# Filler tiles that shift the byte offsets of a mixer layer's matrix operands, on one Trainium2 core

## Chip, core and metric

The kernel runs on one core of a Trainium2 chip. The metric is the device time of one execution in microseconds (us). Engines are named as the profile names them: PE is TensorE's matmul, PEld its weight load, DVE VectorE, ACT ScalarE, POOL GpSimd, SP SyncE, which issues most of the transfers.

## What is computed

The reference is one decoder layer on x of 1024 tokens by 1024 channels, all float32:

```python
h = rms_norm(x, g_pre) * (1.0 + scale) + shift
proj = h @ w_in                      # 1024 x 7704, split into 13 parts
o_fox  = fox_attention(fq, fk, fv, log_f)      # 8 heads of 64, causal, forget gates
o_gla  = rms_norm(gla_chunked(gq, gk, gv, log_a))   # 4 heads, carried state
o_pool = pool_mixer(pu, w_pool, pool_scale)    # windows 2, 4, 8, 16
y_b = (o_b * silu(z_b)) @ w_br_b               # for each of the three branches
merged = sigmoid(m_fox) * y_fox + sigmoid(m_gla) * y_gla + sigmoid(m_pool) * y_pool
out = x + gate * rms_norm(merged @ w_out, g_post)
```

## The kernel before

Each matrix is split into a rounded high part and the rest (`split`, ACT for the high part, DVE for the rest). A product is then three matmuls: high by high, high by low, low by high. `mm3` issues these three for one 128-row slice of the contraction. The first operand of a matmul here is the stationary one, which a weight load (PEld) brings into the array ahead of each matmul; the second is the moving one, streamed as 512 columns in most products.

The stages, in order, with the names that the profile shows for the PSUM tile:

- the start: normalise, transpose and modulate x into `hh` and `hl` (high and low part of h, transposed), with the first products `ps_gq`, `ps_gk`, `ps_n` in between;
- gated linear attention with its projections. `proj_N256` makes tiles `ps_gv` and `ps_fv` of 256 columns, `proj_T` makes tiles of 512 columns (`ps_gq`, `ps_gk`, and `ps_zg` for the first part of z_gla);
- 23 pairs of 128-channel column groups of `w_in` through `seven`, a scheme with seven block products instead of eight. A pair's tiles are `pp_zg`, `pp_pu`, `pp_zp`, `pp_fq`, `pp_fk`, `pp_zf` or `pp_m`; each of its seven products is four slices by three matmuls, so a pair has 84 matmuls of 128x512, and all pairs 1932. The weights `w_*` are prepared by POOL sums (`S_*`), ACT and DVE splits; the moving operands are `hh`, `hl` and the sums `T2`, `T3`, `T4`. Between them, pooling windows (`win`) and the small products `pspl` hang on DVE;
- attention in 128-query blocks (`psL`, `tp`, `po`), with the first branch product `psy` of y_pool woven in;
- `y_tile` for the branches (`psy`, 3 x 192 matmuls of 128x512), then the output product `pso` (360 of 512 columns, 48 of 256) and the final norm.

SBUF tiles lie in pools that are opened and closed as stacks from the left and from the right end of each partition, so a tile's byte offset follows from the sizes of what was opened before it on its side. Left: `cst`, `wp` (weights of `proj_T` and `proj_N256`), `hp` (`hh`, `hl`), `tq`, `tr` (the sums T); later `mA`, `yp` (branch weights `wh_y`, `wl_y`), `oga` (operands `ogh`, `ogl` of two branches), `wo` (`woh`, `wol`). Right: `shr` (the weights `w_*` of `seven`, the attention operands), and later `ogf` and `mB` (operands of the third branch, `ml`). A scheduler sets the order of instructions on each engine from a model of their durations.

Of the kernel before, what the change touches and what calls it, by code (L numbers as in the profile page):

```python
# [8 lines left out]
F32 = mybir.dt.float32  # L9
# [7 lines left out]
P = 128  # L17
# [12 lines left out]
def kernel(  # L30
# [22 lines left out]
    V, A, G, T = nc.vector, nc.scalar, nc.gpsimd, nc.tensor  # L53

    def pool(name, bufs=1, side="left", space=None):
        kw = dict(name=name, bufs=bufs, reuse_waits="tile")
        if space is not None:
            kw["space"] = space
        else:
            kw["side"] = side  # L60
        return tc.tile_pool(**kw)

    def open_pool(name, **kw):
        stack = ExitStack()
        return stack.enter_context(pool(name, **kw)), stack
# [7 lines left out]
    def halves():  # L73
        return ((0, slice(0, HALF)), (1, slice(HALF, S)))


    cst = ctx.enter_context(pool("cst"))
# [4 lines left out]
    def bank(tag, name, shape=(P, HALF)):  # L82
        if tag == "acc":
            return ps_acc.tile(list(shape), F32, tag="acc", name=name, bufs=2)
        return ps_acc.tile(list(shape), F32, tag=tag, name=name, bufs=BANKS[tag])
# [21 lines left out]
    def split(raw, hi, lo, scale=1.0, E=None):  # L107
        i = A.activation(hi, raw, AF.Copy, scale=scale)  # L108
        if scale == 1.0:
            j = (E or V).tensor_tensor(out=lo, in0=raw, in1=hi.bitcast(F32), op=ALU.subtract)  # L110
        else:
            j = V.scalar_tensor_tensor(
                out=lo, in0=raw, scalar=scale, in1=hi.bitcast(F32), op0=ALU.mult, op1=ALU.subtract
            )
        return i, j
# [14 lines left out]
    def load_w_256(src, name):  # L130
        parts = []
        for kh in range(2):
            rows = src[kh * 512 : (kh + 1) * 512, :].rearrange("(k p) e -> p k e", p=P)
            raw = wtile("wr", f"wr_{name}{kh}", F32, (P, 4, 256))
            nc.sync.dma_start(raw, rows)
            hi, lo = (wtile(t, f"{t}_{name}{kh}", shape=(P, 4, 256)) for t in ("wh", "wl"))
            split(raw, hi, lo)
            parts.append((hi, lo))
        return parts

    def mm3(ps, wh, wl, rh, rl, first, last):
        T.matmul(ps, wh, rh, start=first, stop=False)  # L142
        T.matmul(ps, wh, rl, start=False, stop=False)  # L143
        T.matmul(ps, wl, rh, start=False, stop=last)  # L144
# [12 lines left out]
    def proj_N256(col, name, evac):  # L157
        parts = load_w_256(w_in[0, :, col : col + 256], name)
        for st in range(S // P):
            sl = slice(st * P, (st + 1) * P)  # L160
            ps = ps_acc.tile([P, 256], F32, tag="acc", name=f"ps_{name}{st}")
            for k in range(NK):
                wh, wl = parts[k // 4]
                wh, wl = wh[:, k % 4, :], wl[:, k % 4, :]
                T.matmul(ps, hh[k][:, sl], wh, start=(k == 0), stop=False)  # L165
                T.matmul(ps, hh[k][:, sl], wl, start=False, stop=False)  # L166
                T.matmul(ps, hl[k][:, sl], wh, start=False, stop=(k == NK - 1))
            with tc.high_priority():
                evac(st, ps)


    shr, shr_stack = open_pool("shr", side="right")
# [323 lines left out]
    for i in range(3):  # L496
        t = gp.tile([P, 4, 2, 64], F32, tag=f"qbd{i}", name=f"qbd{i}")
# [3 lines left out]
    for i in range(2):  # L501
        t = gp.tile([P, 4, P], F32, tag=f"scs{i}", name=f"scs{i}")
# [180 lines left out]

    gates(0)
    proj_N256(C_GV, "gv0", evac_vg(0))
    gla_unit(0, 0)
    proj_T(C_GQ + P, "gq1", evac_q(1))
    proj_T(C_GK + P, "gk1", evac_k(1))
    gates(1)
    forget_logs()  # L690
    gla_unit(0, 1)
    proj_N256(C_FV, "fv0", evac_vf(0))
    proj_N256(C_GV + 256, "gv1", evac_vg(1))
    rms_gla(0)
    gla_unit(1, 0)
# [14 lines left out]
    sp, sp_stack = open_pool("seven", side="right")  # L710
# [161 lines left out]
    def big(name, dt=F32):  # L872
        brot[0] += 1
        return sh(GT[brot[0] % 2], name, dt=dt)

    def parts_to_dram(t, hi_d, lo_d, name, scale=1.0, hi=None):
        if hi is None:
            hi = big(f"hi_{name}", F32R)
        split(t, hi, t.bitcast(F32R), scale)
        nc.sync.dma_start(hi_d, hi.bitcast(F32))  # L880
        nc.sync.dma_start(lo_d, t)
# [41 lines left out]
    def fin_pool(q, d):  # L923
        def f(j, t):
            g = 2 * q + j
            raw = sp.tile([P, P], F32, tag="wpr", name=f"wpr{g}")
            nc.sync.dma_start(raw, w_pool[0, g])
            wph = sp.tile([P, P], F32R, tag="wph", name=f"wph{g}")
            wpl = sp.tile([P, P], F32R, tag="wpl", name=f"wpl{g}")
            split(raw, wph, wpl)  # L930
            dh, dl = big(f"dh{g}", F32R), big(f"dl{g}", F32R)
            split(d[j], dh, dl)
            for i, hs in halves():
                ps = bank("bd"[i], f"pspl{g}{i}")
                mm3(ps, wph, wpl, dh[:, hs], dl[:, hs], True, True)
                V.scalar_tensor_tensor(out=t[:, hs], in0=ps, scalar=psc[:, g : g + 1], in1=t[:, hs],
                                       op0=ALU.mult, op1=ALU.mult)
            parts_to_dram(t, oph_dram[g], opl_dram[g], f"op{g}")
        return f
# [116 lines left out]
    mA, mA_stack = open_pool("mA")  # L1056
    yp, yp_stack = open_pool("yp")
    oga, oga_stack = open_pool("oga")

    def load_y(src, name):  # L1060
        raw = yp.tile([P, NK, P], F32, tag="wr", name=f"wr_{name}", bufs=2)
        nc.sync.dma_start(raw[:, 0:4, :], src.rearrange("(k p) e -> p k e", p=P))
        hi = yp.tile([P, 4, P], F32R, tag="wh", name=f"wh_{name}", bufs=2)
        lo = yp.tile([P, 4, P], F32R, tag="wl", name=f"wl_{name}", bufs=2)
        split(raw[:, 0:4, :], hi, lo, 0.25)
        return hi, lo
# [157 lines left out]
        y_tile(1, j, "mid", ("d", "b") if j == 8 - KEEP else ("a", "c"))  # L1224
    oga_stack.close()
    wo, wo_stack = open_pool("wo")
    woh, wol = [], []

    def load_wo(k2, n):
# [83 lines left out]
```

## Time and profile before

| what | value |
|---|---|
| median of 3 runs | 1142.23 us (1141.19 to 1147.51) |
| the profiled execution | 1150.32 us, span 1148.6 us |
| PE busy | 1096.8 us, 95% of the span |
| PEld / DVE / ACT / POOL busy | 870.5 / 768.4 / 456.3 / 403.8 us |
| mean granted clock of PE | 0.978 |

A matmul's own duration (some 0.39 us for 512 columns) is longer than the time from its start to the start of the next, since matmuls overlap; the pace is read from starts.

### The profile page before, as it was taken

To read this page: it belongs to the slowest core of one execution; us is meant where nothing else is said; L and a number is where in the kernel's file an instruction comes from. 1 tells how busy PE (TensorE), PEld (TensorE's weight loads), DVE (VectorE), ACT (ScalarE), POOL (GpSimd) and SP (SyncE) were. 2 spreads that over 40 slices of the span, in tenths; PEclk is the share of its full clock that TensorE was granted. 3 is DMA by queue.
4 is the path that set the end of the run, shared out by engine and by line. 5 is a ranking of instruction groups with operands and counts; after the bars stand their busy time and mean duration, and the time that the engine had idled before them with its cause. 6 is when DMAs were issued, how large, how long until landed. Compare 5 with 4: busy or idle time off the path is not lost.

```text
span 1148.6 us, 15822 instructions
## 1 busy us (share of the span) xinstructions
PE 1096.8 (95%) x5812; PEld 870.5 (76%) x5812; DVE 768.4 (67%) x1427; ACT 456.3 (40%) x864; POOL 403.8 (35%) x348
## 2 busy tenths in 40 slices
PE   6899997999998999899999999998998999999997
PEld 4579786988886888688888888875675777677886
DVE  7667799767778677987666564536564668477323
ACT  5235354434534332443434443324443444433211
POOL 4323235033454345445645454411020225343000
PEclk9799999999998999999999999998999999999999
DMA  9810111211332433256653333289949584465332
GB/s 290 227 38 20 37 42 34 65 52 52 116 109 94 149 124 97 74 201 239 220 181 113 128 110 112 88 247 309 234 148 230 182 242 138 165 201 166 110 110 74
DMA packets 109746, 159.81 MB, mean 139 GB/s; under 512 B 7842, under 2 KB 83164, under 8 KB 109668
## 3 DMA queue, kind: packets, MB, share of 16 engines
q1 hardware_dynamic: 109316, 157.99, 45.1%
q8 instruction: 46, 0.75, 0.3%
q10 hardware_dynamic: 352, 0.80, 0.2%
q14 instruction: 32, 0.26, 0.1%
HBM read 113.64 MB, written 45.12 MB: 138 GB/s over the span
## 4 chain that ended last, share of the span: by engine, by line
PE 77%; DVE 11%; DMA 6%; POOL 2%; issue 2%; ACT 2%; SPq 0%; DVEq 0%; ACTq 0%; POOLq 0%
PE pp_m L142 7%; PE pp_m L143 7%; PE pp_m L144 7%; PE po L1105 3%; PE psy L142 3%; PE psy L144 3%; PE psy L143 3%; PE pso L1264 3%; PE pso L1265 3%; PE pso L1263 3%; PE tp L1095 3%; DMA wr_y<-in_w_br_pool_dram 2%; PE psc L605 2%; PE ps_gv L165 1%; PE ps_gv L166 1%
## 5 line engine op out<-in xcount | busy, mean ns | idle before, releaser
L999 POOL TENSOR_SCALAR_AFFINE_SELECT Fd<-F 128x128 f32<-128x128 f32 x64 | 22.9, 359 | 163.4 <-DVE mx L1021 122.6
L143 PE MATMUL psy<-ogl,wh_y 128*128 128x512 f32 x192 | 77.0, 401 | 3.0 <-DMA ogl<-opl_d 3.0
L142 PE MATMUL psy<-ogh,wh_y 128*128 128x512 f32 x192 | 78.0, 410 | 0.4 <-DMA ogh<-oph_d 0.3
L143 PE MATMUL pp_m<-hl,w_m 128*128 128x512 f32 x192 | 75.9, 396 | 0.0
L144 PE MATMUL pp_m<-hh,w_m 128*128 128x512 f32 x192 | 75.9, 396 | 0.0
L142 PE MATMUL pp_m<-hh,w_m 128*128 128x512 f32 x192 | 75.9, 395 | 0.0
L144 PE MATMUL psy<-ogh,wl_y 128*128 128x512 f32 x192 | 75.1, 400 | 0.1
L1028 ACT ACTIVATE t<-t,ng 128x1024 f32<-128x1024 f32 (+3 forms) x64 | 49.6, 776 | 53.6 <-DVE ng L1026 52.4
L110 DVE TENSOR_TENSOR w_m<-wr_m,w_m 128x512 fp32r<-128x512 f32 x36 | 45.1, 1256 | 28.1 <-ACT w_m L108 28.1
L110 DVE TENSOR_TENSOR w_m<-S_m,w_m 128x512 fp32r<-128x512 f32 x48 | 53.9, 1150 | 5.3 <-ACT w_m L108 4.9
L516 POOL TENSOR_TENSOR e<-cum 128x256 f32<-128x256 f32 x24 | 19.9, 829 | 103.1 <-ACT ek L575 30.7
L1095 PE MATMUL tp<-ident,t 128*128 128x128 f32 x288 | 48.8, 286 | 6.8 <-ACT PT L1097 6.7
L1016 DVE CUSTOM_DVE_ANT_0 t<-psL,F 128x512 f32<-128x512 f32 (+2 forms) x80 | 41.0, 523 | 19.9 <-PE psL L1013 14.9
L1264 PE MATMUL pso<-wol,mh 128*128 128x512 f32 (+1 forms) x136 | 51.8, 382 | 0.0
L1265 PE MATMUL pso<-woh,ml 128*128 128x512 f32 (+1 forms) x136 | 51.7, 382 | 0.0
L903 ACT ACTIVATE o_m<-o_m 128x512 f32<-128x512 f32 x48 | 29.1, 630 | 56.5 <-DVE o_m L804 41.4
L1263 PE MATMUL pso<-woh,mh 128*128 128x512 f32 (+1 forms) x136 | 51.4, 379 | 0.0
L1095 PEld LDWEIGHTS tp<-ident,t 128*128 128x128 f32 x288 | 33.8, 143 | 22.3 <-ACT PT L1097 10.4
L1267 DVE TENSOR_TENSOR yo<-pso,gb 128x512 f32<-128x512 f32 (+1 forms) x17 | 11.2, 661 | 55.4 <-ACT jk L1266 55.4
L1105 PE MATMUL po<-PT,vf 128*64 128x256 f32 (+1 forms) x320 | 48.0, 373 | 0.0
L771 POOL TENSOR_TENSOR S_m<-wr_m,wr_m 128x512 f32<-128x512 f32 x12 | 15.6, 1296 | 86.1 <-DMA wr_m<-in_w_in_dram 86.1
L143 PEld LDWEIGHTS psy<-ogl,wh_y 128*128 128x128 f32 x192 | 36.5, 190 | 11.7 <-DMA ogl<-opl_d 4.5
(580 smaller groups left out, 3417.7 us busy)
## 6 DMA issues: line engine op xcount, KB each, us to landing
wr_m<-in_w_in_dram SPq DMA_DIRECT2D x24, 512.0 KB, 4.2
m_d<-o_m SPq DMA_DIRECT2D x24, 512.0 KB, 4.8
m_in<-m_d SPq DMA_DIRECT2D x24, 512.0 KB, 5.5
wa<-in_w_ada_dram SPq DMA_DIRECT2D x16, 512.0 KB, 7.5
xn<-in_x_dram SPq DMA_DIRECT2D x8, 512.0 KB, 6.2
kl<-fkl_d SPq DMA_DIRECT2D x16, 256.0 KB, 10.4
kk<-fkh_d SPq DMA_DIRECT2D x16, 256.0 KB, 6.6
F<-fc_d SPq DMA_DIRECT2D x8, 512.0 KB, 10.3
```

The costliest lines, as they stand in the source:

```text
L110: j = (E or V).tensor_tensor(out=lo, in0=raw, in1=hi.bitcast(F32), op=ALU.subtract)
L142: T.matmul(ps, wh, rh, start=first, stop=False)
L143: T.matmul(ps, wh, rl, start=False, stop=False)
L144: T.matmul(ps, wl, rh, start=False, stop=last)
L903: A.activation(t, t, AF.Tanh, scale=0.5)
L1016: V.tensor_tensor_reduce(out=t[:, c0:e], in0=ps[:, : e - c0], in1=Fb[p, h][:, c0:e], scale=1.0, scalar=-3e38, op0=ALU.subtract, op1=ALU.ma ...
L1028: A.activation(t[:, :W], t[:, :W], AF.Exp, bias=ng[:, 0:1], accum_out=sm)
L1095: T.transpose(tp[:, j, :], t[:, kb * P : (kb + 1) * P], ident)
L1105: T.matmul(po[64 * h : 64 * h + 64, q0:256], vf[p // 2, kb // 4][:, kb % 4, col : col + 64], pts[h, kb // 4][:, kb % 4, q0:256], start=(kb ...
L1263: T.matmul(ps[:, :w], mh[k][:, sl], hi, start=(k == 0), stop=False)
L1264: T.matmul(ps[:, :w], mh[k][:, sl], lo, start=False, stop=False)
L1265: T.matmul(ps[:, :w], ml[k][:, sl], hi, start=False, stop=(k == NK - 1))
```

## The change

Three filler tiles are added that nothing reads: 32 bytes at the right end (`off_r`), and 384 bytes ahead of the operands in `oga` and ahead of the weights in `wo` (`off_a`, `off_w`). Each is cleared by one DVE memset. To make room for them, the raw tile `wpr` of the pooling weights moves from pool `sp` to the two buffers `Fd` of `cst`, which attention uses later.

```diff
+    def filler(pl, nbytes, name):
+        t = pl.tile([P, nbytes // 4], F32, tag=name, name=name)
+        V.memset(t, 0.0)
+
+    off = ctx.enter_context(pool("off", side="right"))
+    filler(off, 32, "off_r")
...
-            raw = sp.tile([P, P], F32, tag="wpr", name=f"wpr{g}")
+            raw = cst.tile([P, P], F32, tag="Fd", name=f"wpr{g}", bufs=2)
             nc.sync.dma_start(raw, w_pool[0, g])
...
     oga, oga_stack = open_pool("oga")
+    filler(oga, 384, "off_a")
...
     wo, wo_stack = open_pool("wo")
+    filler(wo, 384, "off_w")
```

Where the operands of the products of 512 columns lie by the allocator, as byte offset in a partition modulo 512. Slices of a tile step by multiples of 512 bytes and share its value:

| product | matmuls | moving, before | stationary, before | both, after |
|---|---|---|---|---|
| `pp_*` of `seven` | 1932 | 448 (`hh`, `hl`, T) | 480 (`w_*`) | 448 |
| `psy` of two branches | 384 | 64 (`ogh`, `ogl`) | 448 (`wh_y`, `wl_y`) | 448 |
| `psy` of the third branch | 192 | 480 | 448 | 448 |
| `pso` | 360 | 64 (`woh`, `wol`) | 448 (`mh`), 480 (`ml`) | 448 |
| first `ps_gq`, `ps_gk`, `ps_n` | 128 | 448 | 480 | 448 |
| `ps_gq`, `ps_gk`, `ps_zg` of `proj_T` | 192 | 448 | 448 | 448 |
| `psL`, `pspl`, `pb` | 136 | 480 | 480 | 448 |

The products of 256 columns `ps_gv` and `ps_fv` have 448 for both, before and after.

On the queue of SP, in the start, the transfers of modulation weights `wa` stand in a row before. Two of the four `wpr` loads, which stood some 1/4 into the program, now stand among them.

```order
L243 DMA wa_426<-in_w_ada_dram 128x8x128
L135 DMA wr_gv_956<-in_w_in_dram 128x4x256
L243 DMA wa_506<-in_w_ada_dram 128x8x128
L243 DMA wa_508<-in_w_ada_dram 128x8x128
L243 DMA wa_553<-in_w_ada_dram 128x8x128
```

The same place of the changed kernel, whose lines stand 8 further down in this part of the code:

```order
L251 DMA wa_431<-in_w_ada_dram 128x8x128
L135 DMA wr_gv_961<-in_w_in_dram 128x4x256
L251 DMA wa_511<-in_w_ada_dram 128x8x128
L935 DMA wpr_3552<-in_w_pool_dram 128x128
L935 DMA wpr_3594<-in_w_pool_dram 128x128
L251 DMA wa_513<-in_w_ada_dram 128x8x128
L251 DMA wa_558<-in_w_ada_dram 128x8x128
```

Two loads moved ahead of the `wa` loads that follow; the other two kept their place.

On DVE, at the end of the last pair of `pp_m`, the two output sums of the pair stood behind each other before (`v_m` and `o_m` are sums over PSUM tiles of that pair, `PT` belongs to attention):

```order
L1030 TENSOR_SCALAR t_6583<-t_6583,sm_6596 128x896
L804 TENSOR_TENSOR v_m_6628<-pp_m_6615,u_m_6613 128x512
L804 TENSOR_TENSOR o_m_6507<-pp_m_6648,v_m_6628 128x512
L804 TENSOR_TENSOR o_m_6508<-pp_m_6664,u_m_6613 128x512
L1099 COPY PT_6733<-tp_6740 128x4x128
```

The same place of the changed kernel:

```order
L1038 TENSOR_SCALAR t_6588<-t_6588,sm_6601 128x896
L812 TENSOR_TENSOR v_m_6633<-pp_m_6620,u_m_6618 128x512
L174 MEMSET off_a 128x96
L812 TENSOR_TENSOR o_m_6512<-pp_m_6653,v_m_6633 128x512
L812 TENSOR_TENSOR o_m_6513<-pp_m_6669,u_m_6618 128x512
L1108 COPY PT_6740<-tp_6747 128x4x128
```

One memset came between, and it carries no wait of its own. `off_w` stands in the same way between two steps of the last branch, `off_r` is DVE's first instruction. Elsewhere PE's order differs only among the first products of the start, and ACT's and POOL's not at all.

## Rows read from the trace of the kernel before

**Rows 1.** The page: busy time, granted clock by slices, the chain that ended last.
```profile
PE 1096.8 (95%) x5812; PEld 870.5 (76%) x5812; DVE 768.4 (67%) x1427; ACT 456.3 (40%) x864; POOL 403.8 (35%) x348
...
PEclk9799999999998999999999999998999999999999
...
PE 77%; DVE 11%; DMA 6%; POOL 2%; issue 2%; ACT 2%; SPq 0%; DVEq 0%; ACTq 0%; POOLq 0%
```

**Rows 2.** Busy time by engine in one stretch, granted clock, DMA share.
```profile
531.00:768.00 237.00, 237.00 (x1020) 190.89 (x1019) 139.75 (x163) 92.35 (x156) 112.34 (x76) 1.00 0.47 150
```

**Rows 3.** Timeline of PE in the pairs (start, duration): 27 matmuls, first and last.
```profile
607.74 0.40 PE L142 MATMUL pp_m<-T4h,w_m 128*128 128x512 f32 x1
...
613.81 0.40 PE L144 MATMUL pp_m<-hh,w_m 128*128 128x512 f32 x1
```

**Rows 4.** Timeline of PE, output product: 57 matmuls, first and last.
```profile
1069.64 0.40 PE L1265 MATMUL pso<-woh,ml 128*128 128x512 f32 x1
...
1082.71 0.40 PE L1264 MATMUL pso<-wol,mh 128*128 128x512 f32 x1
```

**Rows 5.** Timeline of PE, third branch: 33 matmuls, first and last.
```profile
1010.67 0.40 PE L142 MATMUL psy<-ogh,wh_y 128*128 128x512 f32 x1
...
1018.13 0.40 PE L144 MATMUL psy<-ogh,wl_y 128*128 128x512 f32 x1
```

**Rows 6.** Timeline of PE in ps_zg: products 2, 9, 25 and 48, and what followed.
```profile
271.02 0.39 PE L143 MATMUL ps_zg<-hl,wh_zg 128*128 128x512 f32 x1
...
272.63 0.39 PE L144 MATMUL ps_zg<-hh,wl_zg 128*128 128x512 f32 x1
...
276.26 0.39 PE L142 MATMUL ps_zg<-hh,wh_zg 128*128 128x512 f32 x1
...
281.47 0.40 PE L144 MATMUL ps_zg<-hh,wl_zg 128*128 128x512 f32 x1
281.71 0.62 PE L679 MATMUL pb<-rr,sel 128*128 128x512 f32 x2
```

**Rows 7.** Timeline of PE, 256 columns: ps_gv 24 matmuls, pso 38, first and last.
```profile
88.02 0.28 PE L165 MATMUL ps_gv<-wh_gv,hh 128*128 128x256 f32 x1
...
90.78 0.28 PE L167 MATMUL ps_gv<-wh_gv,hl 128*128 128x256 f32 x1
...
1137.78 0.28 PE L1263 MATMUL pso<-woh,mh 128*128 128x256 f32 x1
...
1142.14 0.28 PE L1265 MATMUL pso<-woh,ml 128*128 128x256 f32 x1
```

**Rows 8.** The chain that ended last (start, duration, what), two places.
```profile
297.49 0.63 ACT w_zg L108
...
449.45 0.68 DVE o_pu L804
```

**Rows 9.** Timeline of PE, where those places end: idle before, and its releaser.
```profile
365.96 0.79 PE L142 MATMUL pp_zp<-T4h,w_zp 128*128 128x512 f32 x1 [3.81 <-DVE o_zp L936]
...
471.48 0.79 PE L142 MATMUL pspl<-dh,wph 128*128 128x512 f32 x1 [2.58 <-DVE o_zp L804]
```

**Rows 10.** The same chain by line, of 768 to 930 and of 930 to 1149.
```profile
by line: DMA wr_y<-in_w_br_pool_dram 15.9%; PE po L1105 15.3%; PE tp L1095 12.2%; DMA kl<-fkl_d 7.1%; PE psy L142 6.9%; PE psy L143 6.9%; PE psy L144 6.6%; PE psL L1013 5.6%; PE psL L1012 5.6%; DMA kk<-fkh_d 4.6%; PE psg L1183 2.7%; DVE t L
...
by line: PE pso L1264 13.7%; PE pso L1265 13.6%; PE pso L1263 13.5%; PE psy L142 10.2%; PE psy L144 10.1%; PE psy L143 9.8%; PE po L1105 6.4%; PE tp L1095 4.3%; DMA wr_y<-in_w_br_fox_dram 3.6%; DVE wl_y L112 2.3%; PE psL L1012 2.2%; PE psL 
```

**Rows 11.** Timeline of DVE and of PE in the fourth pp_m pair.
```profile
592.18 4.14 DVE L110 TENSOR_TENSOR w_m<-S_m,w_m 128x512 fp32r<-128x512 f32 x4 [1.26 <-ACT w_m L108]
...
595.14 0.40 PE L142 MATMUL pp_m<-T2h,w_m 128*128 128x512 f32 x1
```

**Rows 12.** DVE memsets by form (busy us, mean ns, idle before), and the wpr issues.
```profile
L356 DVE MEMSET wn<- 128x512 f32 x1 | 0.5, 485 | 0.1
...
L193 DVE MEMSET one_col<- 128x1 f32 x1 | 0.1, 59 | 0.9 <-PEq L1299 0.9
...
L927 SPq DMA_DIRECT2D wpr<-in_w_pool_dram x4: 333/337/383, 295.8 to 379.7; - x4
```

## Prediction

> **What bounds the kernel now.** I read the page first. PE is busy for 95% of the span at an almost full granted clock, and the chain that ended last is PE for 77% [rows 1]. So the pace of PE's matmuls counts in most of the span, and the question is whether that pace can be other than it is. Busy time and a matmul's own duration don't tell, since neighbours overlap; I therefore went to the timeline of PE and divided stretches without idle time by the number of steps from start to start.
>
> In the pairs of `seven`, 26 steps take 613.81 - 607.74 = 6.07 us, 0.2335 us each [rows 3]. The output product takes 13.07 us for 56 steps, 0.2334 [rows 4]; the third branch 7.46 us for 32 steps, 0.2331 [rows 5]. These have three different distances between the offsets of the moving and the stationary operand (448 and 480; 64 and 448 or 480; 480 and 448), all unequal, and one pace: 0.2333 us.
>
> `ps_zg` is the counter-example that the kernel already holds: the same 128x512 products, both operands at 448. Its products 9 to 25 take 3.63 us for 16 steps, and 25 to 48 take 5.21 us for 23: 0.2265 to 0.227 us [rows 6]. The step behind product 48, where the next weight load reads a tile at 480, is 0.24 us [rows 6]. And it does not start at that pace: products 2 to 9 take 1.61 us for 7 steps, 0.230 [rows 6]. I read this as a rhythm between the moving stream of one matmul and the weight load of the next, which both read SBUF. With equal offsets they fall into step after some eight products and stay so until something else comes between.
>
> **The gain per product.** 0.2333 - 0.2267 = 0.0067 us, if equal offsets are the cause. That the offsets are what differs is my inference: `ps_zg` also keeps its weights in another pool and runs while fewer pairs are under way, but the step behind its last product, with the same neighbours at work, goes back to 0.24. Weights of `ps_zg` step by 512 bytes and its moving operand by 2048, so their distance takes all multiples of 512 without breaking the pace; that is why I expect modulo 512 to be enough. The two bounds for a product that is brought to equal offsets are 0 and 0.0067 us; I take the upper one for unbroken streams, as `ps_zg` is the same instruction, and half of it where other products are woven in [rows 6].
>
> The Trainium skill speaks against any gain: TensorE: Matmul & The Clock Gate, "Step-by-step: what each phase is for", says that PE has two independent SBUF read ports and that loading the next weights takes no read bandwidth from the running matmul. By that rule the offsets would not matter and the time would stay as it was. This trace does not agree, with 0.2267 against 0.2333 us for one kind of instruction [rows 3, 6].
>
> **Where it counts.** 1932 + 576 + 360 = 2868 matmuls of the large stages come from unequal to equal offsets. All of them on the path would give 2868 x 0.0067 = 19.1 us, which is the most. From it I take what does not reach the end:
>
> - The first pairs. From 297.49 the chain leaves PE and runs through ACT, DVE, POOL and the load of `wr_zp` until 365.96, where PE has been waiting for 3.81 us [rows 8, 9]. What PE wins in between only lengthens that wait. PE's last matmul ahead of the wait ends at 365.96 - 3.81 = 362.15, so the stretch is some 64 us, about 270 products at 0.2333. A second such chain runs from 449.45 to 471.48, with a wait of PE of 2.58 us at its end [rows 8, 9]: 19.4 us, about 80 products. 1932 - 350 = 1582 remain, 10.5 us.
> - The rest of the pairs. Between 531 and 768 PE is busy for all of 237 us; DVE has 140, POOL 112, ACT 92 us in it and the DMA share is 0.47 [rows 2], so these engines can follow when a pair takes 19.0 instead of 19.6 us. The thinnest place is the fourth `pp_m` pair: the four splits of `S_m` end at 596.32, the first of them, for the third product, near 593.2 to 593.4 (a quarter of 4.14 us behind 592.18, or a little more), and PE starts that product at 595.14, 1.7 to 1.9 us later [rows 11]. If the weights' side did not get faster by then, the five pairs ahead, 5 x 0.56 = 2.8 us, would use that up and stall PE for 1.1 us; if it does, for 0. I take 0.5. Leaves 10.0.
> - Attention, 768 to 930. `psy` is 20.4% of the chain there [rows 10], 33 us or about 140 products, always broken up by `tp` and `po`; half the gain, 0.5 us.
> - From 930 on. `psy` is 30.1% of 219 us, 66 us or 282 products, 1.9 us; the 360 of `pso` 2.4 us [rows 10].
>
> Together 10.0 + 0.5 + 1.9 + 2.4 = 14.8 us.
>
> **What it costs.** The memsets are 8 and twice 96 columns; between 59 ns for 1 column and 485 ns for 512 [rows 12], together at most 1.5 us if each took the price of the widest and all lay on the path, and 0 if DVE's slack covers them. None waits, and only the one at the end of the pairs sits in front of sums that PE's attention products wait for; I take 0.15. If that cover were gone it would be 0.15 twice. The two `wpr` loads now hold SP for 0.33 to 0.38 us each [rows 12] ahead of six or more `wa` loads in the start: between 0, as these loads wait for buffers that PE frees, and 0.8 us; I take 0.15, nearer to 0. The 48 output products of 256 columns might lose: with equal offsets `ps_gv` runs at 2.76/23 = 0.1200 us, with unequal ones `pso` at 4.36/37 = 0.1178 [rows 7], 48 x 0.0022 = 0.1 us. Sum of costs 0.4 us.
>
> So the gain is 14.8 - 0.4 = 14.4 us: 1150.3 becomes 1135.9 in a profiled execution like this one. That execution lies 8.1 us above the median of the runs, and as the pace of products is the same in any of them I take the difference off the median: 1142.2 - 14.4 = 1127.8 us.
>
> **The rivals.**
>
> - *No effect* (0.06). The offsets are not the cause, or the ports are apart as the rule above has it. For it: only 96 products of `ps_zg` and few others show the fast pace. Against it: the step at 281.47 [rows 6]. Time: 1142.2 + 0.4, 1142.6 us.
> - *Partial* (0.16). The rhythm breaks wherever PSUM banks or operands change, as it takes eight products to form [rows 6]; or only the pairs gain, since `psy` and `pso` have other tile forms. For half of the 14.8 us less the costs of 0.4: 1135.2 us. Against it: product 25 of `ps_zg` begins a new PSUM tile without a break [rows 6].
> - *The weights' side binds* (0.08). In the pairs, 1.7 us of slack in the fourth `pp_m` [rows 11] is gone and PE waits for DVE's and ACT's splits, so that the pairs up to there gain nothing: of the 1582 products some 420 fall away, 2.8 us, time about 1130.1 us in place of the 0.5 us already taken off. This lies within the range.
> - *Slower* (0.03). Equal offsets collide instead of falling into step, as the 256-column products suggest. At 0.0022 us for each of 2868 products [rows 7] it costs 6.3 us: 1148.9 us. It decides from where products of `seven` start more than 0.2333 us apart. Against it stands all of `ps_zg`.
> - *Forecast* (0.67).
>
> By these, faster by over 0.5% (under 1136.5 us, about what a measurement of this kernel can tell from no change) has 0.67 + 0.08 and most of the partial case, 0.90; slower by over 0.5% has 0.03; the same 0.07. The lower end of the range is all 19.1 us and 2 us for waits in attention, where one slice shows a granted clock of 0.8 [rows 1] that could as well be full: 1121. The upper end takes in most of the partial case: 1136.
>
> **What would show it.** Right: in the pairs, `pso` and `psy` of the changed kernel, starts 0.2267 us apart; the stretch of twelve `pp_m` pairs shorter by some 6.7 us; the wait at the first `pp_zp` longer by about 1.8 us, at the second `pspl` by 0.5. Wrong: starts still at 0.2333 (no effect), at 0.230 (a rhythm that never forms), or at 0.2267 with new idle time of PE in front of `pp_m` products, released by DVE or ACT. The sum would be wrong, too, if the start or attention came out several us different for their clock or order alone.

## The result

The changed kernel takes 1132.57 us in the median (1131.56 to 1143.19, 7 runs), beside 1146.27 us of the kernel before on the same chip: a ratio of 0.989, 95% interval 0.9856 to 0.9925. A second timing of it, beside other runs of before, gave 1137.06 to 1147.58 us, 0.9915 (0.9883 to 0.9947). So it is faster by about 1%, 10 to 14 us, against a forecast of 14.4; the time itself lies 4.8 us above the 1127.8 forecast, inside the range of 1121 to 1136. The profiled execution takes 1131.79 us, with a span of 1130.1.

The page of the changed kernel, in the order of [rows 1] (busy time, granted clock by slices, the chain that ended last):

```profile
PE 1078.4 (95%) x5812; PEld 868.9 (77%) x5812; DVE 770.6 (68%) x1430; ACT 455.1 (40%) x864; POOL 406.3 (36%) x348
...
PEclk8899998999999999999999999999899999999999
...
PE 66%; DMA 13%; DVE 12%; POOL 3%; ACT 2%; issue 2%; SPq 1%; DVEq 0%; ACTq 0%; POOLq 0%
```

PE still does 5812 matmuls and is still busy for 95%, but for 18.4 us less. That share tells as little as before; the starts tell it. First the timeline of PE in the twelve `pp_m` pairs (start, duration), the counterpart of [rows 3], 20 matmuls:

```profile
581.67 0.39 PE L142 MATMUL pp_m<-T4h,w_m 128*128 128x512 f32 x1
...
585.98 0.39 PE L143 MATMUL pp_m<-hl,w_m 128*128 128x512 f32 x1
```

19 steps in 4.31 us, 0.2268 us each; before it was 0.2335. The output product, counterpart of [rows 4], 57 matmuls:

```profile
1054.81 0.39 PE L1274 MATMUL pso<-wol,mh 128*128 128x512 f32 x1
...
1067.50 0.39 PE L1273 MATMUL pso<-woh,mh 128*128 128x512 f32 x1
```

12.69 us for 56 steps, 0.2266. The third branch, counterpart of [rows 5], where products of the output with 256 columns are woven in:

```profile
999.76 0.39 PE L142 MATMUL psy<-ogh,wh_y 128*128 128x512 f32 x1
...
1001.57 0.39 PE L144 MATMUL psy<-ogh,wl_y 128*128 128x512 f32 x1
1001.80 0.28 PE L1273 MATMUL pso<-woh,mh 128*128 128x256 f32 x1
1001.91 0.28 PE L1274 MATMUL pso<-wol,mh 128*128 128x256 f32 x1
1002.03 0.40 PE L142 MATMUL psy<-ogh,wh_y 128*128 128x512 f32 x1
1002.26 0.40 PE L143 MATMUL psy<-ogl,wh_y 128*128 128x512 f32 x1
1002.50 0.39 PE L142 MATMUL psy<-ogh,wh_y 128*128 128x512 f32 x1
1002.73 0.40 PE L143 MATMUL psy<-ogl,wh_y 128*128 128x512 f32 x1
```

Eight steps up to 1001.57 take 1.81 us, 0.226; behind the two of 256 columns the three steps from 1002.03 to 1002.73 take 0.70 us, 0.233 again. The rhythm is lost there and has to form anew. Over all dense steps this branch runs at 0.2278 us and the one before it at 0.2294, so these two have a part of the gain only.

The stretch of the twelve `pp_m` pairs, in the view by window (its length, then busy time of PE, PEld, DVE, ACT, POOL, granted clock, DMA share, GB/s), counterpart of [rows 2]:

```profile
527.30:757.30 230.00, 230.00 (x1017) 190.56 (x1016) 139.32 (x166) 92.65 (x158) 114.27 (x76) 1.00 0.49 155
```

PE is busy throughout, as before, and the stretch is 230.0 us instead of 236.7. The whole span, from the first matmul of one stage to that of the next (the pairs, in all three, from their 19th matmul, 4.1 to 4.2 us behind their first), in the profile of before and in two profiles of the changed kernel (the second is from experiment 9):

| stage | before | after | after, second profile |
|---|---|---|---|
| start, linear attention, `ps_zg` | 298.7 | 299.2 | 300.0 |
| first eleven pairs | 232.0 | 228.0 | 229.1 |
| twelve `pp_m` pairs | 236.7 | 230.0 | 231.4 |
| attention, up to the second branch | 154.0 | 148.5 | 150.4 |
| two branches `psy` | 143.6 | 142.7 | 142.8 |
| `pso`, from its second tile | 77.2 | 75.2 | 75.2 |
| tail | 6.4 | 6.5 | 6.5 |
| span | 1148.6 | 1130.1 | 1135.3 |

### The profile page after: what moved, and what is told of

Its sections match the earlier page's. It is cut to its first block, busy times and chain, and to the rows that moved or that the text cites. A ratio compares the mean times of both kernels' runs of the same rounds, so it can differ in the third digit from the quotient of the medians.

```text
span 1130.1 us, 15820 instructions
## 1 busy us (share of the span) xinstructions
PE 1078.4 (95%) x5812; PEld 868.9 (77%) x5812; DVE 770.6 (68%) x1430; ACT 455.1 (40%) x864; POOL 406.3 (36%) x348
## 4 chain that ended last, share of the span: by engine, by line
PE 66%; DMA 13%; DVE 12%; POOL 3%; ACT 2%; issue 2%; SPq 1%; DVEq 0%; ACTq 0%; POOLq 0%
PE pp_m L142 7%; PE pp_m L144 7%; PE pp_m L143 7%; PE po L1114 3%; PE pso L1274 3%; PE pso L1275 3%; PE pso L1273 3%; PE tp L1104 2%; PE psc L613 2%; PE psy L142 2%; PE psy L143 2%; PE psy L144 2%; DMA wr_y<-in_w_br_pool_dram 2%; DMA wro<-in_w_out_dram 2%; DMA wr_zp<-in_w_in_dram 2%
## 5 line engine op out<-in xcount | busy, mean ns | idle before, releaser
L142 PE MATMUL pp_m<-hh,w_m 128*128 128x512 f32 x192 | 74.7, 389 | 0.0
L144 PE MATMUL pp_m<-hh,w_m 128*128 128x512 f32 x192 | 74.7, 389 | 0.0
L144 PE MATMUL psy<-ogh,wl_y 128*128 128x512 f32 x192 | 74.0, 394 | 0.2 <-DVE wl_y L112 0.2
L110 DVE TENSOR_TENSOR w_m<-wr_m,w_m 128x512 fp32r<-128x512 f32 x36 | 42.7, 1189 | 34.4 <-ACT w_m L108 34.4
L110 DVE TENSOR_TENSOR w_m<-S_m,w_m 128x512 fp32r<-128x512 f32 x48 | 56.5, 1205 | 4.4 <-ACT w_m L108 4.2
## 6 DMA issues: line engine op xcount, KB each, us to landing
F<-fc_d SPq DMA_DIRECT2D x8, 512.0 KB, 10.1
```

## Experiments

The theory: PE's pace at 512 columns is set by the distance between the offsets of the moving and the stationary operand; equal offsets let two neighbouring matmuls fall into a rhythm of 0.2267 us, others stay at 0.2333. The main rival: something else that the change moved (an order, a pool, a neighbour of the fillers), and with it the question whether modulo 512 is the right measure.

**1. The pace by itself.** A kernel that computes no part of the layer: one tile of 49152 bytes per partition, from which every configuration takes the operands of 60 matmuls, one behind the other, with chosen offsets and nothing beside them.

```python
for j in range(60):
    m0 = (mo - 128) % 512 // 4 + 512 * (j % 8)            # moving at offset mo
    s0 = 6144 + (so - 128) % 512 // 4 + 128 * (j * 5 % 44) # stationary at so
    T.matmul(acc[:, 0:w], big[:, s0 : s0 + P], big[:, m0 : m0 + w], ...)
```

> This kernel computes no part of the layer: it runs 60 matmuls of 128x512 (or 128x256) back to back for each of 34 choices of offsets of the two operands, from one tile filled with x, and writes a constant block. Theory 1 (equal offsets modulo 512): with a distance of 0 starts are 0.2267 us apart wherever the pair lies (448, 480, 0, 256, 464, 452), with every other distance from 32 to 480, and with 4, 8 and 16 bytes, 0.2333. Rival (alignment to 64 bytes of either operand is what counts, since 448 is a multiple of 64 and 480 is not): distances 64, 128, 192 and so on run at 0.2267, and the equal pairs at 480, 464 and 452 at 0.2333. Rival (the ports are apart): all alike. For 256 columns both theories leave open whether 0.1178 or 0.1200 us belongs to equal offsets; if the profile of before is a guide, equal is 0.1200 and unequal 0.1178.

Timeline of PE; each row is one configuration of 60 matmuls (start, time to the end of the last one). The first two are 256 columns at distance 0 and 32, then 512 columns at distance 0, 32, 64 and 256, then equal offsets at 480, at 464 and at 452:

```profile
72.65 7.35 PE L47 MATMUL chd<-big 128*128 128x256 f32 x60
79.84 7.17 PE L47 MATMUL che<-big 128*128 128x256 f32 x60
...
115.33 13.83 PE L47 MATMUL cdj<-big 128*128 128x512 f32 x60
129.00 14.15 PE L47 MATMUL cdk<-big 128*128 128x512 f32 x60
142.99 13.91 PE L47 MATMUL cdl<-big 128*128 128x512 f32 x60
...
226.78 13.77 PE L47 MATMUL cdr<-big 128*128 128x512 f32 x60
...
338.18 13.78 PE L47 MATMUL cez<-big 128*128 128x512 f32 x60
...
379.02 14.15 PE L47 MATMUL cecz<-big 128*128 128x512 f32 x60
393.01 14.51 PE L47 MATMUL cedz<-big 128*128 128x512 f32 x60
```

At distance 32 the 59 steps take 14.15 - 0.40 = 13.75 us, 0.233; at 256 they take 13.77 - 0.39 = 13.38, 0.2268. Over the last 30 steps of each, distances 0 and 256 have 0.2267 us, 64 and 320 have 0.2289, 160 and 416 have 0.2345, and the other ten multiples of 32 have 0.2333. The list from 256 on repeats that from 0: the period is 256 bytes, not the 512 of the prediction. Equal offsets are 0.2267 at 448, 480, 0 and 256, but 0.2333 at 464 and 0.2392 at 452, so equality was not enough at these two, which are no multiples of 32. The rival of an alignment to 64 bytes is out: distance 64 is not at 0.2267, and equal offsets at 480 are. At distance 0 behind a stream of 256 columns, the first 20 steps average 0.2298 (13.83 in place of 13.77), and by the starts in the trace the first ten go from 0.224 to 0.241: the rhythm has to form. Behind streams of 512 columns it formed within one step at distance 256, so the eight products of [rows 6] are no fixed number. At 256 columns equal offsets are the slowest (0.1200) and distance 32 the fastest (0.1167).

**2 to 4. Parts of the change.** Experiment 2 leaves out the two fillers of 384 bytes, experiment 3 the filler of 32 bytes, and experiment 4 makes that one 16 bytes:

```diff
 # 2                                # 3                                # 4
-    filler(oga, 384, "off_a")      -    filler(off, 32, "off_r")      -    filler(off, 32, "off_r")
-    filler(wo, 384, "off_w")                                          +    filler(off, 16, "off_r")
```

> Only the 32 bytes on the right (and the move of wpr) remain. Theory 1: pairs at 0.2267 us and the third branch too, the two other branches at 0.2333, and the output product at 0.2333 as its operands stay 64 and 448; gain about 11 us of the whole change's 12 to 14, ratio near 0.990 to 0.992 of before. Alignment to 64 bytes: everything at 0.2267, since 64 and 448 are both multiples of 64; the whole gain.

1137.58 us, ratio 0.9909 (0.9878 to 0.9940). The pairs run at 0.2267, and so does what the filler at the right end makes equal in the branches (`psy` of the third branch at 0.2280); the second branch stays at 0.2323 and `pso` at 0.2333. The gain sits where the equal offsets are. The 2 to 3 us that the branches and `pso` should add can't be seen in a ratio with this interval, only in the stages.

> Only the two fillers of 384 bytes (and the move of wpr) remain. Theory 1: pairs stay at 0.2333 us, two branches run at 0.2267, the third at 0.2333, the output product in between since two of its three matmuls have equal offsets; gain 2 to 3 us, ratio near 0.998. Alignment: no product changes its pace, ratio 1.000. If the memsets or the move of wpr were behind the gain instead, it would show here whole.

1148.12 us, ratio 1.0004 (0.998 to 1.0028): no gain. The pairs stay at 0.2333, though two branches run at about 0.230. The miss is `pso`: two of its three matmuls (with `mh`) have equal offsets now, the third (with `ml`) has not, and I had expected a pace in between. Timeline of PE, 37 matmuls:

```profile
1090.03 0.39 PE L1273 MATMUL pso<-woh,ml 128*128 128x512 f32 x1
1090.26 0.40 PE L1271 MATMUL pso<-woh,mh 128*128 128x512 f32 x1
1090.49 0.40 PE L1272 MATMUL pso<-wol,mh 128*128 128x512 f32 x1
...
1098.43 0.39 PE L1273 MATMUL pso<-woh,ml 128*128 128x512 f32 x1
```

8.40 us for 36 steps, 0.2333 for all three kinds. One unequal matmul in three takes the gain from the other two.

> The whole change, with 16 instead of 32 bytes on the right: the same instructions, the operands of the pairs 16 bytes apart (448 and 464). Theory 1: pairs at 0.2333 us, nearly all of the gain gone, ratio 0.998. If the hardware looks at pieces of 32 bytes or more: 464 lies in the same 32 bytes as 448, pairs at 0.2267 and ratio 0.989 as with the change. If something other than offsets made the gain, it stays too, but with pairs at 0.2333.

1135.24 us, ratio 0.991 (0.9879 to 0.9941), pace 0.2267. The allocator gave the neighbours the same offsets as with 32 bytes, so this is the change once more and says nothing on 16 bytes; experiment 1 did (distance 16: 0.2284).

**5. A second sweep**, again with nothing of the layer: equal offsets with one unequal matmul (480) in 3, in 6 and in 20, and more distances.

```diff
+    """kind, moving offset, stationary offsets in turn, columns in turn"""
...
+    out.append(("m", 448, [448] * 2 + [480], [512]))
+    out.append(("m", 448, [448] * 5 + [480], [512]))
+    out.append(("m", 448, [448] * 19 + [480], [512]))
```

> Again no part of the layer: 60 matmuls back to back for each choice, from one tile filled with x, and a constant block as output. Groups: 256 columns at distances of 0 to 224 bytes; 384 columns at 0, 32 and 128; 512 columns with one unequal stationary operand (480 in place of 448) in 3, in 6 and in 20; 512 columns broken by two matmuls of 128 or three of 256; 512 columns at distances 252, 248, 4, 12 and 256. Theory of a rhythm with a period of 256 bytes that forms over some steps: one unequal in 3 never lets it form, 0.2333 us for all three; one in 20 costs some ten slower steps each time, near 0.230; breaks cost likewise. Rival (each matmul pays for its own distance): one in 3 gives (2 x 0.2267 + 0.2333)/3 = 0.2289, one in 20 gives 0.2270. For 256 columns the profile of the first sweep is expected again: 0.1200 at 0, 0.1167 at 32, and something between elsewhere; at 256 bytes and 512 columns 0.2267.

Timeline of PE, these three and distance 256 as the measure:

```profile
196.06 14.14 PE L54 MATMUL cmt<-big 128*128 128x512 f32 x60
210.05 13.96 PE L54 MATMUL cmu<-big 128*128 128x512 f32 x60
223.85 13.82 PE L54 MATMUL cmv<-big 128*128 128x512 f32 x60
...
318.83 13.77 PE L54 MATMUL cdcz<-big 128*128 128x512 f32 x60
```

Over the last 30 steps 0.2333, 0.2300 and 0.2276 us. If each matmul had its own price, one in three would give 0.2267 + 0.0066 / 3 = 0.2289, and one in six 0.2278. Each unequal one therefore costs about as much as three: by the starts in the trace, the step up to it takes 0.235 us and the next three 0.228, 0.232 and 0.231, and then the pace is 0.2267 again. That is a rhythm and not a price by the piece, and it explains experiment 3. For one in 20 I had expected near 0.230; the rhythm came back sooner than the ten steps that I had in mind. Two more configurations break equal offsets by other widths: behind two matmuls of 128 columns the second step of 512 is at 0.231 and the third at 0.227, behind three of 256 columns five steps are slower (0.228 to 0.236). A distance of 4 bytes gave 0.2333 here and 0.2267 in experiment 1, behind another stream: at this distance what ran before may decide, which no run shows further.

**6. Modulo 256 in the kernel.** The fillers on the left are cut from 384 to 128 bytes, which puts the operands of two branches and of `pso` 256 bytes apart modulo 512.

```diff
-    filler(oga, 384, "off_a")
+    filler(oga, 128, "off_a")
...
-    filler(wo, 384, "off_w")
+    filler(wo, 128, "off_w")
```

> The whole change, with 128 instead of 384 bytes ahead of the operands in oga and wo: these lie at 192 then, 256 bytes from the stationary ones at 448. If the period is 256 bytes, as the first sweep says, the output product runs at 0.2267 us as in the change and the two branches too, ratio 0.989. If it takes equality modulo 512 in the kernel, as the change was made for, both stay at 0.2333 and 3 us of the gain are missing, ratio 0.9915.

1140.66 us beside 1150.01, ratio 0.9921 (0.9892 to 0.9949). `pso` runs at 0.2267 and the branches at 0.2282 to 0.2296, as with 384 bytes. 256 bytes are enough in the kernel too.

**7. The moved load by itself.** All fillers out, `wpr` still in the buffers of `cst`.

```diff
-    off = ctx.enter_context(pool("off", side="right"))
-    filler(off, 32, "off_r")
...
-    filler(oga, 384, "off_a")
...
-    filler(wo, 384, "off_w")
```

> Only the move of wpr to the Fd buffers, no filler. If its price is what was taken (0.15 us, at most 0.8), the ratio is 1.000 within its interval, and the stretches of the profile up to the first 256-column projection and through the pairs are as before within 1 us, all products at 0.2333. If the move were what shortens the kernel or shortens attention, the time falls here by several us with the pace unchanged. Attention, which took 154 us with 20.5 us at the half clock before and 148.5 with 6.8 us after, should follow its own time at the half clock, at about 0.45 us for each us, whatever the offsets.

1149.82 us, ratio 1.0004 (0.9978 to 1.003); up to attention no stage moves by over 0.6 us, and the pace is 0.2333. Moving the loads costs nothing that can be seen, and gains nothing either.

**8 and 9. Could the projections gain too?** Experiment 1 has 256 columns fastest at distance 32. A filler of 32 bytes ahead of the projection weights, and one of 224 ahead of `hh` (so that the pairs keep equal offsets modulo 256), give `ps_gv` and `ps_fv` that distance, at the price of unequal offsets for `proj_T`. Experiment 9 is the changed kernel as its partner.

```diff
     filler(off, 32, "off_r")
+    filler(wp, 32, "off_wp")
+    filler(hp, 224, "off_hp")
```

> The changed kernel with a filler of 32 bytes ahead of the weights of the projections and one of 224 bytes ahead of hh and hl. The products of 256 columns (ps_gv, ps_fv, 768 of them) then have the moving operand 32 bytes above the stationary one (modulo 256), the 192 products of proj_T (ps_gq, ps_gk, ps_zg) 32 below, and everything else stays at equal offsets modulo 256. If the distance modulo 256 sets the pace at either width as the two sweeps showed: ps_gv and ps_fv go from 0.1200 to 0.1167 us, ps_zg from 0.2267 to 0.2333, the pairs and all later stages keep 0.2267. 768 x 0.0033 = 2.6 us less in the stretch from the first ps_gv to ps_zg (190.9 us in the changed kernel) if PE bounds it, and 192 x 0.0067 = 1.3 us more, of which 0.6 in the stretch of ps_zg: about 1.2 us faster than the changed kernel, 0.1%, ratio to the kernel before lower by 0.001. Rival: at 256 columns the sweep's difference belongs to unbroken streams of one tile, and in the projections, where splits and transfers run beside, ps_gv stays at 0.1200: then 1.3 us slower than the changed kernel.

> The changed kernel once more, on the same chip as the version with shifted projections, as its partner. Ratio to the kernel before 0.988 to 0.992; attention (from the last pp_m to the first psy of the branches) between 145 and 155 us, moving by some 0.4 to 0.5 us for each us in which PE has the lower clock there, all other stages within 0.5 us of the first profile of the changed kernel. If the 5.5 us by which attention was shorter in that first profile came from the offsets and not from the clock, attention is near 148 us again whatever the clock does.

Timeline of PE in `ps_gv`, 49 matmuls of experiment 8:

```profile
90.78 0.28 PE L165 MATMUL ps_gv<-wh_gv,hh 128*128 128x256 f32 x1
...
96.38 0.28 PE L165 MATMUL ps_gv<-wh_gv,hh 128*128 128x256 f32 x1
```

and 58 matmuls of experiment 9:

```profile
89.14 0.28 PE L165 MATMUL ps_gv<-wh_gv,hh 128*128 128x256 f32 x1
...
95.97 0.28 PE L165 MATMUL ps_gv<-wh_gv,hh 128*128 128x256 f32 x1
```

5.60 / 48 = 0.1167 against 6.83 / 57 = 0.1198 us: the pace follows the distance as the sweep has it, and `ps_zg` goes to 0.2332. But the stretch from the first `ps_gv` to `ps_zg` shrinks by 0.4 us only (190.9 to 190.5) instead of 2.6: summed over all their steps `ps_gv` gains 1.0 us and `ps_fv` 0.1, where longer steps between the dense ones take the rest back. `ps_zg` takes 0.6 us more. 1137.11 us (ratio 0.9902, 0.9865 to 0.9939) against 1137.06: it does not beat the change. Experiment 9 missed in its stages: all but attention were to be within 0.5 us of the first profile, and three were longer, the start by 0.8, the first eleven pairs by 1.1 and the twelve `pp_m` pairs by 1.4. Attention in it is 150.4 us at a granted clock of 0.98, between the 148.5 of the first profile and the 154.0 of before; more on this below.

## Why the prediction was right

**The cause** is the one it named. Unbroken streams run at 0.2267 us where the offsets are brought together and at 0.2333 where they are not, in the kernel (experiments 2, 3, 6) and with nothing else running (experiment 1). *No effect* and *slower* are out: the same 60 matmuls take 13.77 us at distance 256 and 14.15 at distance 32. The rule that stood behind *no effect* is the Trainium skill's, in TensorE: Matmul & The Clock Gate, "Step-by-step: what each phase is for", that loading the next weights takes no read bandwidth from the running matmul; by it the distance would not matter, and 13.77 against 14.15 us disagrees. That it is the two reads of SBUF which get into each other's way stays my reading: the runs show the pace by distance, not what happens inside. Two details of the prediction were off. Modulo 512 was too strict (256 does), and the rhythm breaks more easily than I took it for: it lives through a change of the PSUM tile, as [rows 6] said, but not through one unequal matmul in three.

**The pairs**, predicted at 10.0 us, gained 10.7 in the profile after and 8.2 in the second one. The two chains did absorb what I took off: from the start of the pairs to the first `pp_zp` the time is 67.3 us before and 67.4 after. But the wait in front of `pp_zp` did not grow by 1.8 us as I had it; it fell from 3.81 [rows 9] to 3.49. Timeline of PE, matmuls with a wait (idle before, its releaser), two more of before:

```profile
352.15 0.50 PE L143 MATMUL pspl<-dl,wph 128*128 128x512 f32 x1 [1.26 <-DVE dl L110]
...
358.17 0.50 PE L142 MATMUL pspl<-dh,wph 128*128 128x512 f32 x1 [0.61 <-DVE o_zp L804]
```

and after:

```profile
352.73 0.80 PE L143 MATMUL pspl<-dl,wph 128*128 128x512 f32 x1 [2.52 <-DVE dl L110]
...
366.57 0.80 PE L142 MATMUL pp_zp<-T4h,w_zp 128*128 128x512 f32 x1 [3.49 <-DVE o_zp L944]
...
464.35 0.51 PE L142 MATMUL pspl<-dh,wph 128*128 128x512 f32 x1 [2.51 <-ACT dh L108]
...
469.77 0.50 PE L142 MATMUL pspl<-dh,wph 128*128 128x512 f32 x1 [1.03 <-DVE o_zp L812]
```

What PE won came out at the earlier wait, that of the first `pspl` for `dl`, 2.52 us (before 1.26, and 0.61 at another one behind it, which is gone). And behind that wait the next seven matmuls, up to 355.86, run at the lower of the two granted clocks, 1.2 GHz (the 0.80 us of the first row, where 0.4 is usual); before, the clock there was the full 2.4 GHz. The lower clock takes PE 1.5 us more for the same matmuls, ahead of a wait that has room for it. Together 0.65 + 1.5 - 0.3 = 1.85, the 1.8 us that I had looked for in one place. The same at the second chain: 1.46 became 2.51, 2.58 became 1.03 (in the second profile it stayed at 2.58).

**The fourth `pp_m` pair** was rightly the thinnest place. The 1.7 to 1.9 us of [rows 11] are mostly used up. Timeline of DVE (the first split alone) and of PEld, before:

```profile
592.18 1.23 DVE L110 TENSOR_TENSOR w_m<-S_m,w_m 128x512 fp32r<-128x512 f32 x1 [1.26 <-ACT w_m L108]
...
595.38 0.19 PEld L144 LDWEIGHTS pp_m<-T2h,w_m 128*128 128x128 f32 x1
```

and after:

```profile
588.29 1.22 DVE L110 TENSOR_TENSOR w_m<-S_m,w_m 128x512 fp32r<-128x512 f32 x1 [1.25 <-ACT w_m L108]
...
590.06 0.19 PEld L144 LDWEIGHTS pp_m<-T2h,w_m 128*128 128x128 f32 x1
```

DVE makes the low part of the weights, which the third matmul of `mm3` is the first to read (L144); I had measured up to the first, which reads ACT's high part. So the room was 595.38 - 593.41 = 2.0 us, and of it 590.06 - 589.51 = 0.55 are left. In the second profile nothing is left. Timeline of PE there, in the second product of the pair, one ahead of the one I had named:

```profile
590.33 0.50 PE L144 MATMUL pp_m<-hh,w_m 128*128 128x512 f32 x1 [0.52 <-DVE w_m L110]
```

What is late is not DVE but the load behind it. The view of tile `wr_m` for this pair and the one ahead of it, time from the issue of its loads to landing, after:

```profile
DMA to landing us min/median/max: 3.7/4.7/5.8
```

and in the second profile:

```profile
DMA to landing us min/median/max: 3.6/5.6/7.5
```

One load landed 1.7 us later, and the stretch took 231.4 instead of 230.0. Of the six profiles with the fast pace in the pairs, the three without a stall have 230.0 us, and their slowest load of this view lands after 5.7 to 6.2 us; the three with one have 231.2 to 231.9, and theirs after 7.2 to 7.5. That is 0.75 us in the mean of the six, where I took off 0.5: the right place and about the right size, but the wrong link, since I had put it on the splits. Why the load lands later in some executions stays open.

**The branches** were sized too high: 1.9 us predicted, 0.9 measured. 282 products at the full gain was wrong in two ways. Woven products keep the rhythm from holding (0.2294 us in the second branch), and in the third, where the pace gains 1.0 us, PE now waits for the splits of the next branch weights. Waits of PE from 990 to 1049 after (waited for, us, times, longest), where before had none in this branch:

```profile
PE psy L142 <- ACT wh_y L108: 0.3, 1, 0.3
PE psy L144 <- DVE wl_y L112: 0.2, 1, 0.2
```

**The chain** shows the same shift. By line, from 915 to 1130 after, for [rows 10]:

```profile
by line: PE pso L1274 13.4%; PE pso L1275 13.4%; PE pso L1273 13.3%; DMA wro<-in_w_out_dram 10.6%; PE po L1114 6.5%; PE psy L142 6.2%; PE psy L144 5.8%; PE psy L143 5.8%; DVE wol L110 4.6%; PE tp L1104 4.1%; ACT woh L108 2.9%; PE psL L1020 
```

`psy` is down from 30.1% to 17.8%, and the loads of `w_out`, not in that row before, have 10.6%: a part of the branches is no longer bound by PE alone.

**`pso`** gave 2.0 us in its stretch (2.2 over all its steps), where 2.4 was predicted; the stretch holds 312 of the 360 products, and 38 of the 48 of 256 columns, which lose slightly under the 0.1 predicted (0.1193 us a step in place of 0.1179). The **costs** of 0.4 us can't be told from nothing: experiment 7 has none for the loads. The three memsets take 65, 138 and 138 ns. The first of the two `wpr` loads in the start holds SP for 1.98 us, not the 0.33 to 0.38 of [rows 12], so that cost was sized from the wrong rows, though nothing in the time shows it. The start up to the pairs took 0.5 and 1.3 us more in the two profiles, but 0 more in experiment 2 and 3.3 more in experiment 3, which lacks the filler of the pairs, so no cost of the change can be read there either.

**Attention** gained 5.5 us in the profile, where I had said 0.5. The view by window over attention (the third field from the end is the granted clock, the mean over its two levels): before, after, and experiment 6, which has the fast pace too.

```profile
767.40:921.40 154.00, 141.73 (x853) 99.80 (x852) 92.25 (x371) 68.11 (x153) 26.72 (x48) 0.93 0.83 230
```

```profile
757.30:905.70 148.40, 136.18 (x853) 96.32 (x852) 93.28 (x370) 67.51 (x153) 27.28 (x48) 0.98 0.84 238
```

```profile
762.50:917.10 154.60, 141.30 (x852) 100.35 (x851) 92.45 (x371) 67.74 (x153) 26.64 (x48) 0.93 0.81 229
```

At a granted clock of 0.93 attention takes 154.0 us before and 154.6 with the fast pace; at 0.98 it takes 148.4, and in experiment 4, at 1.00, 145.1. The time falls as the clock rises, but not by the clock alone: at 0.98 experiment 8 has 147.0 and experiment 9 150.4, and experiment 7, with the offsets of before, has 153.8 at 0.96, 2 to 3 us more than was expected of it by its clock. A gain of 0.5 us by the offsets can't be seen in this scatter. The profiles are 18.5 us apart, the medians 13.7 and 10.5; the 5.5 us of attention are of the size of that gap. Whether a denser PE also makes the low clock rarer stays open: the shares differ from execution to execution, and nine profiles are too few.

In sum: without attention the stages gained 13.0 us in the first and 9.7 us in the second profile, against 13.9 predicted; the forecast is at the upper end of what was measured, and the terms that were too high are the branches (1.0 us) and, in half of the profiles, the fourth `pp_m` pair. In the second profile the start (0.8 us) and the first eleven pairs (1.1 us) took longer as well; PE's waits between 294 and 480 add up to 11.8 us there against 10.1 in the first. And of the 4.8 us by which the time misses 1127.8, 4.0 are the base: the kernel before has a median of 1146.27 over seven runs, and 1142.23 over the three from which the forecast was taken.

## What to carry to other kernels

When one matmul follows another without idle time, look at the distance from start to start of the same instruction in several places; if it differs, compare where the operands lie. A filler of a few bytes cost nothing that could be seen here and can be worth 3% of a dense stretch, but all matmuls of the stretch have to agree, since one in three that doesn't takes the whole gain. And a stretch that PE leaves faster needs its loads earlier: margins of 1 to 2 us that a profile shows may lie within the scatter of a transfer.

## What was not expected of the hardware

- The pace repeats every 256 bytes of distance. It is not only fast or slow: 0.2267, 0.2289, 0.2333 and 0.2345 us by distance at 512 columns.
- Equal offsets gave 0.2267 us at the four multiples of 32 bytes that were tried (448, 480, 0, 256), but 0.2333 at 464 and 0.2392 at 452.
- The best distance depends on the width: at 512 and 384 columns it is 0 (0.2267 and 0.1733 us, against 0.2333 and 0.1767 at 32), at 256 columns 0 is among the worst (0.1200, as 40 and 96) and 32 or 48 the best (0.1167).
